# Loading the experts' first matrix in runs of 4 KB, with transposes of every second column

## The chip, the core and the metric

The kernel runs on one core of a Trainium2 chip. Its engines work side by side, each through its own queue in order: TensorE (PE; its weight loads are shown apart as PEld), VectorE (DVE), ScalarE (ACT), GpSimd (POOL) and SyncE (SP), which issues most DMAs. The metric is the device time of one execution in microseconds, as the median of several runs; less is better.

## The reference

The reference is one layer of a backbone over 1024 latent tokens of 1024 features, with 256 tokens of context. A first part mixes tokens (a gated recurrence and a spatial gating); it isn't touched. The second part is a mixture of experts, with 64 experts of which each token takes eight, and a shared expert that all tokens take:

```python
def swiglu(h, w_gu, w_down):
    gate, up = jnp.split(h @ w_gu, 2, axis=-1)
    return (jax.nn.silu(gate) * up) @ w_down

def expert_block(acc, blk):            # in moe_ffn, for each block of an expert's tokens
    tok, wts, e = blk
    out = swiglu(h_pad[tok], w_gu[e], w_down[e])
    return acc.at[tok].add(out * wts[:, None].astype(out.dtype)), None

return acc[:N] + swiglu(h, w_sh_gu, w_sh_down)
```

`w_gu[e]` is 1024 x 512 in f32 (gate and up side by side), `w_down[e]` 256 x 1024. All is float32.

## The kernel before

The token mixing fills roughly the first 920 us of the profile. Then come the units of the experts. The shared expert has eight units of 128 tokens; while they run, the routing is worked out: experts are ranked by how many tokens chose them, and each rank has a fixed number of rows, in tiles of at most 128, which gives 100 routed tiles, from 128 rows down to 16. Experts with many and with few rows alternate. Units with more than 128 rows have two tiles. The program is fixed; only the expert's number and the row indices are read at run time.

`step(n)` is a pipeline of three: the rows of unit n come in, unit n - 1 goes through the first matrix, unit n - 2 through the second.

*Weights.* `Weights.load` brings an expert in as six parts of 512 KB, four of `gu` (256 rows of 512 columns each) and two of `down`, into eight rotating buffers `er` of 128 partitions x 2 x 512. SyncE issues them, mostly in pairs, and waits for a buffer to be free; for the shared expert GpSimd issues them. `Weights.split` makes two tiles of each part, a rounded one `eh` (ScalarE, line 123) and the remainder `el` (VectorE, line 126), so that a product of f32 accuracy is three quick products: `eh` by the rounded rows, `el` by the rounded rows, `eh` by the rows' remainder (lines 1113 to 1115).

*Rows.* GpSimd gathers the rows of a tile by index from `h2x` in DRAM into `gx` (line 1092), 1088 values per row, the last 64 being the routing weights. VectorE takes the row's weight out of them (`wj`, line 1098), the first instruction that waits for the gather. `rows_in` transposes the 1024 features on TensorE, eight transposes of 128 columns each into `px` (line 1071), and splits the result into `x`, again with lines 123 and 126. In a transpose `gx` is the weight that is loaded and `ident` moves.

*Products.* `unit_up` accumulates over eight blocks k of 128 features. For a unit of up to 128 rows the weights' 512 columns move (lines 1113 to 1115); for a larger one the rows move (lines 1128 and 1129) and VectorE adds two halves of the result (`up`, line 1132). In the middle of it stands `mid`, which transposes the products of the unit before (`pt`, line 1147). `unit_down` multiplies with the second matrix (`pd`) and GpSimd adds the result to `acc` in DRAM with an indirect DMA (line 1166).

So on TensorE there follow one another: transposes of the next tile's rows, half of the products of the present unit, `pt` of the unit before, the other half, and `pd`. On VectorE `wj` of a coming tile stands ahead of parts of `el` and of the split `x`, so a gather that is late holds these up. On GpSimd adding and gathering DMAs alternate.

A contraction over 1024 features doesn't depend on which 128 of them stand in block k, as long as the rows of the weights and the columns that are transposed agree.

One other line reads with a step. Line 1373, in the routing, multiplies half-precision one-hot tiles that hold eight values side by side and takes one in eight, so that neighbouring columns lie 16 bytes apart:

```python
oa = ep.tile([P, NTT, 8], F16, name=f"oa{i}", tag="eh", bufs=12)
ob_ = ep.tile([P, P, 8], F16, name=f"ob{i}", tag="el", bufs=12)
TE.matmul(pix, ob_[:, :, k], oa[:, :, k], start=(i + k == 0), stop=(i == 7 and k == 7))
```

Of the kernel before, what the change touches and what calls it, by code (L numbers as in the profile page):

```python
# [18 lines left out]
DRAM = bass.MemoryType.DRAM  # L19
# [9 lines left out]
# experts, by descending count, with rows for more than 16 * j tokens  # L29
STEPS = (64, 64, 64, 63, 60, 53, 46, 39, 33, 28, 19, 15, 12, 10, 7, 7, 3, 3, 3, 2, 2, 1, 1, 1)  # L30
TSTEPS = STEPS[::8]  # and with more than j tiles of 128 rows
# [5 lines left out]
def layer(ctx: ExitStack, tc, x, c, cx, c_ctx, w_ada, b_ada, g_pre_mix, g_post_mix, g_pre_ffn, g_post_ffn, w_in,  # L37
# [14 lines left out]
    # tiles that pass from one phase to the other  # L52
# [43 lines left out]
    # vectors over features, one feature per partition  # L96
# [9 lines left out]
    def rsqrt(pool, ss, n, mul, nm):  # L106
        """1/sqrt(ss*mul + EPS) of a [128, n] tile: bit-level seed and three Newton steps."""
        v = pool.tile([P, n], F32, name=f"rv{nm}", tag="rv", bufs=3)
        i = pool.tile([P, n], I32, name=f"ri{nm}", tag="ri", bufs=3)
        y = pool.tile([P, n], F32, name=f"ry{nm}", tag="ry", bufs=4)  # L110
        t = pool.tile([P, n], F32, name=f"rt{nm}", tag="rt", bufs=3)
        V.tensor_scalar(v, ss, mul, EPS, op0=OP.mult, op1=OP.add)  # L112
        V.tensor_scalar(i, v.bitcast(I32), 1, None, op0=OP.arith_shift_right)  # L113
        V.tensor_scalar(y.bitcast(I32), i, -1.0, float(0x5F3759DF), op0=OP.mult, op1=OP.add)  # L114
        for _ in range(3):
            V.tensor_tensor(t, y, y, op=OP.mult)  # L116
            V.scalar_tensor_tensor(t, t, -0.5, v, op0=OP.mult, op1=OP.mult)  # L117
            V.scalar_tensor_tensor(y, t, 1.5, y, op0=OP.add, op1=OP.mult)  # L118
        return y
# [15 lines left out]
    # ================= phase 1 =================  # L135
# [85 lines left out]
    def ada_first(m, fill=iter(())):  # L221
        """Columns m * 512 and up of shift (m < 2) and scale (m >= 2), one feature per partition: the sum over each fourth of
        the rows goes to a group of columns of the tensor engine, where four run side by side."""
        ps = phg(f"pad_{m}")
        for k0 in (0, 4):
            was = [(t2 if m == 1 else pj)(f"wa{m}{k}") for k in range(k0, k0 + 4)]
            for g in range(4):
                last = SP.dma_start(was[g], w_ada[(k0 + g) * P:(k0 + g + 1) * P, m * 512:(m + 1) * 512])
            mm = None
            for g in (3, 0, 1, 2):  # L230
                with tc.issue_after(mm.ins) if mm else ExitStack():
                    i = TE.matmul(ps[32 * g:32 * g + 32], scl32[:, k0 + g], was[g], start=(k0 == 0), stop=(k0 == 4),
                                  tile_position=(0, 32 * g))
                mm = mm or i
            with tc.issue_after(i.ins):
                for _ in range(4):
                    next(fill, None)
        mrow = t2(f"mrow{m}")
        V.tensor_copy(mrow, ps)
        pada = ptr(f"pada{m}", (P, 4, 2))  # L240
        for j in range(4):
            TE.matmul(pada[:, j], mrow[:, j * P:(j + 1) * P], sel2, start=True, stop=True)
        n = m * 4
        for s in range(2):
            if m < 2:
                V.tensor_tensor(B1[:, n:n + 4, s], pada[:, :, s], vt[:, 24 + n:28 + n], op=OP.add)
            else:
                V.tensor_tensor(A1[:, n - 8:n - 4, s], pada[:, :, s], vt[:, 24 + n:28 + n], op=OP.add)
                V.tensor_tensor(A1[:, n - 8:n - 4, s], A1[:, n - 8:n - 4, s], vt[:, 8 + n:12 + n], op=OP.mult)
        return last.ins  # L250
# [6 lines left out]
    def wide(col, nm, al, kps=range(4)):  # L257
        """512 columns of w_in, split: [k] -> (h, l), each [128, 512]."""
# [50 lines left out]
    # in the order of need: half of the shifts and scales, of the modulated tokens and of the weights of the values, and the  # L309
    # products of these; the other halves  # L310
# [25 lines left out]
    def narrow(w, col, nm, nk=KB):  # L336
        """128 columns of w, split: h, l, each [128, nk, 128]."""
# [7 lines left out]
    def tokrows(w, si, i, nm):  # L345
        """[128 tokens, 512] of the modulated tokens times 512 columns of w_in."""
        ps = pmm(f"ps{nm}")
        for k in range(KB):
            tokpart(ps, w, si, i, k)
        return ps  # L350

    def featrows(hw, si, nm):
        """[128 features, tokens of a segment]."""
# [24 lines left out]
    # lower bounds: first entry of the softmax over two  # L378
# [32 lines left out]
    def sigmoids(h, r):  # L411
        """Forget gates to (sigmoid(z), sigmoid(-z)); query to silu."""
# [17 lines left out]
    def gates(hs, d, si, sp, sm, q):  # L430
        """Decayed keys and queries of 512 columns in one direction: one head's segment or two heads' context."""
# [16 lines left out]
        # chunk-level exponents within a block of 128: FQ, FK, L64, L32, Tot  # L448
# [31 lines left out]
        # keys decayed to the end of their chunk  # L480
# [31 lines left out]
    def to_block(g):  # L512
        """Keys decayed to the end of their block of 128, queries from its start, in place."""
# [14 lines left out]
    def scores(h, si, gf, gb):  # L528
        """A^T[s, t] of both directions for the four 128-blocks of a segment."""
# [40 lines left out]
    def hgrn(h, pr):  # L570
# [11 lines left out]
        # states before each block  # L582
# [146 lines left out]
    def gates_out(js):  # L729
        """Output gate of the recurrence (4 blocks) and gate of its branch (8 blocks), before their nonlinearities."""  # L730
# [115 lines left out]
    def choose(i, s_, r):  # L846
        """Chosen experts of a tile of tokens (mbf), how often each is chosen up to it (cum), and the weights."""
# [10 lines left out]
        # sum of the two largest of each group of eight  # L858
# [12 lines left out]
        # the four largest groups, then the eight largest experts, ties by index  # L871
# [10 lines left out]
        # weights of the chosen experts  # L882
# [8 lines left out]
    def out_x1(i, al):  # L891
        """The first sub-layer's residual of a tile of tokens."""
# [22 lines left out]
    def out_h2(i, x1, pool, sq):  # L915
        """The second sub-layer's input, in place."""
# [12 lines left out]
    def route_in(i, h2, wr, pr, tr, f, s_):  # L929
        """Scores of a tile of tokens."""  # L930
# [9 lines left out]
    def second():  # L940
        """All but the second half of the last tile; returns that."""
# [34 lines left out]
    # rows of each rank's slot, and its first row  # L976
# [28 lines left out]
    # ================= experts =================  # L1005
# [25 lines left out]
    class Weights:  # L1031
        """An expert's weights: gu [1024, 512] and down [256, 1024] in DRAM, in six parts, loaded and then split."""
# [5 lines left out]
        def load(self, n=6, q=SP):  # L1038
            for kp in range(self.nload, min(self.nload + n, 6)):
                raw = wp.tile([P, 2, 512], F32, name=f"er{self.nm}{kp}", tag="er", bufs=8)  # L1040
                if kp < 4:
                    last = q.dma_start(raw, self.gu(kp * 256, 256).rearrange("o (k p) f -> p (o k) f", p=P))
# [22 lines left out]
    def rows_in(gx, R, off, x2, nm):  # L1065
        """Rows of one tile, transposed and split, to columns off and up."""
        n = 4 if R > 64 else 8
        for k0 in range(0, KB, n):
            pt = epst(f"px{nm}{k0}")
            for k in range(n):  # L1070
                TE.transpose(pt[:, k * R:(k + 1) * R], gx[0:R, (k0 + k) * P:(k0 + k + 1) * P], ident[0:R, 0:R])  # L1071
# [5 lines left out]
    def unit_in(rows, slot, nm):  # L1077
        """Brings in the rows of a unit: (index column, number of rows) of its tiles; the second tile when told."""
# [27 lines left out]
    def unit_up(u, wg, nm, mid=None):  # L1106
        """silu(gate) * up of a unit's rows: by row for up to 128, else transposed."""
# [33 lines left out]
    def unit_act(u, a, nm):  # L1141
        """The products of a unit, transposed and split."""
# [28 lines left out]
    # units of rows, in order: the shared expert, which starts the sums, then the experts by descending count  # L1171
# [28 lines left out]
    def advance(s, n):  # L1200
        """The next n parts of an expert are split, and as many of the expert after it loaded."""
# [12 lines left out]
    def step(n):  # L1214
        """Rows of unit n come in, unit n - 1 goes up, unit n - 2 down."""
# [22 lines left out]
    # ================= routing, among the tiles of the shared expert =================  # L1238
# [50 lines left out]
    # positions within each expert, by token  # L1289
# [10 lines left out]
    # experts by descending count  # L1300
# [24 lines left out]
    # rows of each expert: its slot's tiles first, then blocks after all slots  # L1325
# [16 lines left out]
    # jump of the row number for positions past the slot  # L1342
# [20 lines left out]
    # tokens by row: products of one-hot rows and columns, eight of each token side by side  # L1363
# [17 lines left out]
    # expert and slot of each block past the slots  # L1381
# [25 lines left out]
    # the residual, for the end  # L1407
# [6 lines left out]
    # blocks past the slots, as many as the counts need  # L1414
# [14 lines left out]
    # ================= output =================  # L1429
# [39 lines left out]
```

## Time and profile before

| | |
|---|---|
| median of 3 runs | 2037.6 us |
| the three runs | 2026.79, 2037.6, 2038.34 us |
| span of the profiled execution | 2039.7 us |
| TensorE busy over the span | 1879.4 us (92%) |
| VectorE, ScalarE, GpSimd busy | 1303.0, 1081.4, 375.4 us |
| mean granted TensorE clock | 0.961 |
| moved by DMA | 412.95 MB, mean 202 GB/s |

The profiled execution is told by its span alone, from its first to its last instruction; it is one execution, and the times of the runs come from others. [...] A matmul that is shown as busy overlaps the next one, so that from its duration alone it isn't seen how quickly they follow each other.

### The profile page before, as it was taken

How to read it: one execution, taken by the hardware profiler on the slowest of the kernel's cores; microseconds unless marked ns; L12 is line 12 of the kernel's file. 1: busy time of each engine (PE TensorE's matmuls, PEld its weight loads, DVE VectorE, ACT ScalarE, POOL GpSimd, SP SyncE). 2: the span in 40 equal slices, each digit the busy share in tenths (PEclk: the TensorE clock that was granted, in tenths of full speed). 3: DMA queues.
4: the chain of work that ended last, by engine and by line, in shares of the span. 5: the costliest groups of instructions: out<-in, count | busy, mean ns of one | idle time of the engine just before them, and what ended most of it. 6: DMA issues, size and time to landing. Idle time of an engine off the chain costs nothing. (4 is left out here: it accounts for less than half of the span.)

```text
span 2039.7 us, 31209 instructions
## 1 busy us (share of the span) xinstructions
PE 1879.4 (92%) x10809; PEld 1493.2 (73%) x10810; DVE 1303.0 (64%) x2915; ACT 1081.4 (53%) x1823; POOL 375.4 (18%) x232
## 2 busy tenths in 40 slices
PE   6999999999999998998999999998999989999990
PEld 3787788878887776876677777776867777787770
DVE  5532867578535577778456776676756757576655
ACT  2437555364122225224447777676766767676652
POOL 0000000000000000000013344243433324432423
PEclk9999999999999998998899999999999989999995
DMA  9241212124016778444359999899989979899965
GB/s 325 84 124 42 63 63 74 58 68 128 19 31 205 227 247 260 154 151 158 128 179 295 315 302 299 238 316 282 295 256 276 320 236 318 285 286 297 322 187 185
DMA packets 224288, 412.95 MB, mean 202 GB/s; under 512 B 21624, under 2 KB 79544, under 8 KB 224128
## 3 DMA queue, kind: packets, MB, share of 16 engines
q1 hardware_dynamic: 199808, 336.70, 48.8%
q0 software_dynamic: 23488, 73.17, 14.7%
q8 instruction: 85, 1.39, 0.3%
q10 hardware_dynamic: 832, 1.08, 0.2%
q14 instruction: 75, 0.61, 0.1%
HBM read 351.18 MB, written 71.58 MB: 207 GB/s over the span
## 5 line engine op out<-in xcount | busy, mean ns | idle before, releaser
L126 DVE TENSOR_TENSOR el<-er,eh 128x1024 fp32r<-128x1024 f32 x384 | 458.0, 1219 | 52.1 <-ACT eh L123 47.2
L123 ACT CAST eh<-er 128x1024 fp32r<-128x1024 f32 x384 | 390.7, 1052 | 30.8 <-PE pg L1115 16.8
L1166 POOL DMA_INDIRECT acc<-y,idx x100 | 185.3, 1853 | 497.8 <-ACT y L1162 112.4
L1092 POOL DMA_INDIRECT gx<-h2x,idx x100 | 165.6, 1656 | 223.9 <-DVE idx L1380 102.0
L1162 ACT ACTIVATE y<-pd,wt 128x512 f32<-128x512 f32 (+7 forms) x200 | 136.9, 685 | 88.3 <-PE pd L133 46.2
L1113 PE MATMUL pg<-eh,x 128*128 128x512 f32 (+5 forms) x384 | 161.4, 420 | 0.0
L1114 PE MATMUL pg<-el,x 128*128 128x512 f32 (+5 forms) x384 | 153.5, 400 | 0.0
L1115 PE MATMUL pg<-eh,x 128*128 128x512 f32 (+5 forms) x384 | 153.5, 400 | 0.0
L1098 DVE SCALAR_TENSOR_TENSOR wj<-rank,gx 128x64 f32<-128x64 f32 (+7 forms) x100 | 21.7, 217 | 156.9 <-DMA gx<-h2x,idx 150.5
L1071 PEld LDWEIGHTS px<-ident,gx 128*128 128x128 f32 (+7 forms) x800 | 79.6, 140 | 22.4 <-issue 2.9
L1071 PE MATMUL px<-ident,gx 128*128 128x128 f32 (+7 forms) x800 | 90.0, 253 | 0.3
L555 POOL MEMSET dg<- 128x128 f32 x8 | 1.6, 205 | 461.4 <-PE pk L523 199.5
L1132 DVE TENSOR_TENSOR up<-pg,up 128x160 f32<-128x160 f32 (+5 forms) x104 | 34.8, 334 | 79.8 <-ACT up L1131 79.8
L1115 PEld LDWEIGHTS pg<-eh,x 128*128 128x128 f32 (+5 forms) x384 | 66.4, 173 | 24.5
L1113 PEld LDWEIGHTS pg<-eh,x 128*128 128x128 f32 (+5 forms) x384 | 67.1, 175 | 20.1
L1114 PEld LDWEIGHTS pg<-el,x 128*128 128x128 f32 (+5 forms) x384 | 67.0, 175 | 18.9
L131 PE MATMUL pd<-eh,swh 128*128 128x512 f32 (+5 forms) x192 | 76.0, 396 | 0.0
L133 PE MATMUL pd<-eh,swl 128*128 128x512 f32 (+5 forms) x192 | 75.7, 395 | 0.0
L132 PE MATMUL pd<-el,swh 128*128 128x512 f32 (+5 forms) x192 | 75.6, 394 | 0.0
L1186 POOL DMA_DIRECT2D sx<-h2x x1 | 0.8, 781 | 393.7 <-DVE rtz L117 393.7
L1131 ACT COPY up<-pg 128x160 f32<-128x160 f32 (+5 forms) x104 | 31.0, 298 | 56.4 <-PE pg L1129 55.6
L126 DVE TENSOR_TENSOR x<-px,x 128x512 fp32r<-128x512 f32 (+3 forms) x91 | 52.3, 613 | 10.2 <-ACT x L123 10.2
(1094 smaller groups left out, 5271.2 us busy)
## 6 DMA issues: line engine op xcount, KB each, us to landing
er<-in_w_expert_gu_dram SPq DMA_DIRECT2D x256, 512.0 KB
er<-in_w_expert_down_dram SPq DMA_DIRECT2D x128, 512.0 KB
wr_ad<-in_w_ada_dram SPq DMA_DIRECT2D x64, 256.0 KB
wa<-in_w_ada_dram SPq DMA_DIRECT2D x32, 256.0 KB
wrga<-in_w_in_dram SPq DMA_DIRECT2D x12, 512.0 KB
gsp<-go SPq DMA_DIRECT2D x24, 256.0 KB
wrc<-in_w_in_dram SPq DMA_DIRECT2D x8, 512.0 KB
wrf<-in_w_in_dram SPq DMA_DIRECT2D x8, 512.0 KB
```

Source lines behind the costliest of these rows:

```text
L123: A.copy(h, src)
L126: V.tensor_sub(l, src, h.bitcast(F32))
L131: TE.matmul(ps, ah, bh, start=(i == 0), stop=False)
L132: TE.matmul(ps, ah, bl, start=False, stop=False)
L133: TE.matmul(ps, al, bh, start=False, stop=(i == n - 1))
L1071: TE.transpose(pt[:, k * R:(k + 1) * R], gx[0:R, (k0 + k) * P:(k0 + k + 1) * P], ident[0:R, 0:R])
L1092: G.indirect_dma_start(out=gx[0:R], out_offset=None, in_=h2x, in_offset=bass.IndirectOffsetOnAxis(ap=ic[0:R], axis=0), bounds_check=T - 1, ...
L1113: TE.matmul(pg[0:C], ah, bh, start=(i == 0), stop=False)
L1114: TE.matmul(pg[0:C], ah, bl, start=False, stop=False)
L1115: TE.matmul(pg[0:C], al, bh, start=False, stop=(i == KB - 1))
L1162: A.activation(y[0:R, hf * 512:hf * 512 + 512], pd[0:R], AF.Copy, scale=1.0 if wt is None else wt[0:R])
L1166: G.indirect_dma_start(out=acc, out_offset=bass.IndirectOffsetOnAxis(ap=ic[0:R], axis=0), in_=y[0:R], in_offset=None, compute_op=OP.add, b ...
```

## The change

A part of `gu` is 256 rows of 2 KB that lie one behind the other in DRAM. Before, partition p takes rows p and 128 + p of the part, two runs of 2 KB. Now it takes rows 2p and 2p + 1, which are one run of 4 KB. The blocks k = 2 kp and 2 kp + 1 of the contraction thus hold the even and the odd features of 256 neighbouring ones, and the transposes take every second column to match. The same holds for the shared expert, whose weights and rows go through the same functions, and for the loop over blocks past the fixed tiles.

```diff
             for kp in range(self.nload, min(self.nload + n, 6)):
                 raw = wp.tile([P, 2, 512], F32, name=f"er{self.nm}{kp}", tag="er", bufs=8)
                 if kp < 4:
-                    last = q.dma_start(raw, self.gu(kp * 256, 256).rearrange("o (k p) f -> p (o k) f", p=P))
+                    last = q.dma_start(raw, self.gu(kp * 256, 256).rearrange("o (p k) f -> p (o k) f", p=P))
...
             for k in range(n):
-                TE.transpose(pt[:, k * R:(k + 1) * R], gx[0:R, (k0 + k) * P:(k0 + k + 1) * P], ident[0:R, 0:R])
+                c0 = (k0 + k) // 2 * 256 + k % 2
+                TE.transpose(pt[:, k * R:(k + 1) * R], gx[0:R, c0:c0 + 255:2], ident[0:R, 0:R])
```

Besides, comments are dropped, which moves line numbers by two behind this place. The instructions of each engine stand in the same order as before, one for one; what differs is the pattern that these loads and these transposes read.

## Rows read from the trace of the kernel before

**Rows 1.** Experts' stretch: PE, PEld, DVE, ACT, POOL busy; clock, DMA share, GB/s.

```profile
1030.00:1966.00 936.00, 883.25 (x4868) 705.35 (x4867) 634.76 (x1031) 646.80 (x1023) 340.75 (x193) 0.97 0.90 282
```

**Rows 2.** Waits of TensorE from 1050 us: total us, times, longest.

```profile
PE pt L1147 <- DVE x L126: 26.9, 12, 4.9
PE pg L1128 <- DVE up L1132: 20.5, 14, 2.8
PE pt L1147 <- DVE x__15325 L126: 4.9, 1, 4.9
```

**Rows 3.** Tile `er`: idle time of an engine before it, by what ended it.

```profile
  DMA er<-in_w_expert_down_dram: 0.3, 1
```

**Rows 4.** Waits of all engines: VectorE behind gathers; total us, times, longest.

```profile
DVE wj L1098 <- DMA gx<-h2x,idx: 150.5, 43, 8.2
```

**Rows 5.** Timeline around one late gather: start, us, instruction, idle before.

```profile
1383.69 2.08 POOL L1092 DMA_INDIRECT gx<-h2x,idx  x1 [0.30 <-PE pd L133]
...
1392.24 0.23 DVE L1098 SCALAR_TENSOR_TENSOR wj<-rank,gx 128x64 f32<-128x64 f32 x1 [7.40 <-DMA gx<-h2x,idx]
...
1394.27 0.58 PE L1147 MATMUL pt<-ident,sw 96*128 96x96 f32 x2 [4.55 <-DVE x L126]
```

**Rows 6.** TensorE in two short stretches: busy, granted clock, DMA share, GB/s.

```profile
974.20:977.00 2.80, 2.80 (x10) 0.50 0.93 285
1394.30:1397.00 2.70, 2.70 (x8) 0.50 0.97 272
```

**Rows 7.** DMA view, 960 to 962 us: packets; queue with packets, MB, share.

```profile
DMA packets 409, 0.77 MB, mean 386 GB/s; under 512 B 32, under 2 KB 32, under 8 KB 409
...
q1 hardware_dynamic: 409, 0.77, 99.9%
```

**Rows 8.** DMA view, 968 to 970 us.

```profile
DMA packets 222, 0.82 MB, mean 408 GB/s; under 512 B 23, under 2 KB 23, under 8 KB 222
...
q1 hardware_dynamic: 222, 0.82, 101.2%
```

**Rows 9.** Timeline of TensorE: groups of eight transposes with 96, 128, 16 rows.

```profile
1451.13 0.82 PE L1071 MATMUL px<-ident,gx 96*128 96x96 f32 x8
...
1463.83 1.03 PE L1071 MATMUL px<-ident,gx 128*128 128x128 f32 x8
...
1467.58 0.66 PE L1071 MATMUL px<-ident,gx 16*128 16x16 f32 x8
```

**Rows 10.** Matmuls by line and shape: busy us, mean ns, idle before.

```profile
L1071 PE MATMUL px<-ident,gx 128*128 128x128 f32 x376 | 48.7, 272 | 0.0
L1373 PE MATMUL small<-oa,ob 128*128 128x164 f16 x64 | 20.1, 477 | 0.0
L1071 PE MATMUL px<-ident,gx 96*128 96x96 f32 x80 | 9.1, 250 | 0.1
...
L1071 PE MATMUL px<-ident,gx 80*128 80x80 f32 x80 | 7.5, 234 | 0.1
L1071 PE MATMUL px<-ident,gx 112*128 112x112 f32 x56 | 6.5, 258 | 0.0
...
L1071 PE MATMUL px<-ident,gx 16*128 16x16 f32 x40 | 3.3, 211 | 0.0
```

**Rows 11.** Timeline of TensorE at three places: strided and dense products.

```profile
970.27 1.93 PE L1373 MATMUL small<-oa,ob 128*128 128x164 f16 x6
...
973.33 2.57 PE L1373 MATMUL small<-oa,ob 128*128 128x164 f16 x8
...
976.12 0.63 PE L1113 MATMUL pgs<-ehs,x2s 128*128 128x512 f32 x1
976.55 0.63 PE L1114 MATMUL pgs<-els,x2s 128*128 128x512 f32 x1
...
1504.17 0.39 PE L1113 MATMUL pg<-eh,x 128*128 128x512 f32 x1
1504.40 0.39 PE L1114 MATMUL pg<-el,x 128*128 128x512 f32 x1
```

## The prediction

> **What bounds the kernel now.** I began with the busy time of the experts' stretch, 1030 to 1966 us, because both edits act there. TensorE is busy for 883 of 936 us at a granted clock of 0.97 [rows 1]; the DMA engines are busy for 0.90 of it. Two resources near their limit, so the next views had to say which one the other waits for. Who waits for whom on TensorE: only two waits of weight, 26.9 us in 12 waits of `pt` behind VectorE's `x`, and 20.5 us in 14 waits of `pg` behind VectorE's `up` [rows 2]. No wait for a weight load is among them. The view of the tile `er`, into which the loads go, shows the other side: its first reader, ScalarE's cast, stood idle for the landing of such a load once, for 0.3 us [rows 3]. So the weight stream is early and TensorE sets the pace, interrupted when VectorE is late. Where VectorE is late it is often for a gather of rows: 150.5 us in 43 waits [rows 4]. One of them is followed through: at 1392.24 VectorE has waited 7.40 us for a gather, the split `x` of the previous rows stands behind it in VectorE's queue, and TensorE's `pt` starts after 4.55 us of idle time [rows 5], in a stretch whose granted clock from 1394.3 to 1397 is 0.50 [rows 6]. That chain is the only way I see by which a quicker weight stream can reach the end of the kernel.
>
> **The load.** 256 expert loads of 512 KB are changed (64 experts with four parts of `gu` each), and four of the shared expert's. Each goes from 256 runs of 2 KB to 128 runs of 4 KB. The price of both kinds of run can be read off two stretches in which SyncE's queue q1 has the engines to itself. From 960 to 962 us there are 409 packets, 32 of them under 512 B, so 377 runs in 0.77 MB, which is 2.04 KB each [rows 7]; 16 engines busy 99.9% of 2 us are 31.97 us, or 84.8 ns a run. From 968 to 970 us there are 222 less 23, so 199 runs in 0.82 MB, 4.1 KB each, in 32.4 us, or 163 ns a run [rows 8]. Two runs of 2 KB cost 170 ns and one of 4 KB 163: a saving of 7 ns, 4%. Over 256 loads it is 256 x 128 x 7 / 16 = 14 us of every DMA engine's time, in a stretch where the engines have about 94 us to spare already. Nobody waits for these landings, so by itself this is worth nothing on the path. SyncE issues the same number of DMAs in the same order. What it can do is let gathers land sooner. The gather followed above took 8.5 us from its issue at 1383.69 to its use; 4% of that is 0.35 us. TensorE waits behind VectorE's `x` 12 times, which makes 4 us. I take -4 us, with bounds of 0 (nothing lands sooner) and -30 (below, under the rivals).
>
> [...]
>
> **The transposes.** Each tile of rows is transposed by eight instructions in which 128 columns of `gx` are loaded as weights and the identity moves past them. The edit leaves their number and order; the 128 columns now lie 8 bytes apart, not 4. No operation of the trace reads so, thus bounds from the nearest rows. First what a transpose costs now, from groups of eight in a row on TensorE's timeline: with 128 rows eight last 1.03 us and the last one 0.272, so they follow each other at (1.03 - 0.272) / 7 = 0.108 us; with 96 rows at (0.82 - 0.25) / 7 = 0.081; with 16 rows at (0.66 - 0.211) / 7 = 0.064 [rows 9, 10]. With many rows the moving identity sets the pace; the floor of 0.064, which doesn't fall with the rows any more, I put down to the weight load.
>
> Then what a stride costs. One line has one: L1373 moves 164 half-precision columns that lie 16 bytes apart. Six take 1.93 us and one of them 0.477 (the mean of all), so they follow each other at 0.291 us; eight take 2.57 us from 973.33 on, so 0.299, and from 974.2 on the granted clock is 0.50 there [rows 6, 10, 11]. That is 1.8 ns a column. An ordinary product with 512 adjacent f32 columns follows the last one at 0.23 us (1504.17 to 1504.40), which is also 1.8 ns for 16 bytes, and at 0.43 us under the clock of 0.50 (976.12 to 976.55) [rows 6, 11]. So the strided read doesn't follow TensorE's clock and the dense one, away from the half clock, sits at the same 1.8 ns. Both fit an estimate: moving on by 16 bytes in a partition takes 1.8 ns, whatever part of them is used. For 128 f32 columns this is 32 steps and 0.058 us dense, just under the floor of 0.064, and 64 steps and 0.115 us at every second column; with the same 0.006 on top, 0.122 us a transpose.
>
> The sum by shape [rows 10]: with 128 rows 376, and 8 x 8 for the shared expert's tiles, are 440, at 0.122 - 0.108 = 0.014 us, 6.2 us; 56 with 112 rows at 0.027 (0.095 now, interpolated), 1.5; 80 with 96 rows at 0.041, 3.3; 80 with 80 rows at 0.052 (0.070 now, interpolated), 4.2; the shapes from 64 rows down to 16, which are what is left of the 100 routed tiles with 8 each, 800 - 376 - 56 - 80 - 80 = 208, at 0.058, 12.1. That is 27 us on TensorE's own queue. The lower bound is 0, since the load may go on at its present pace; a gain I exclude, as no read gets shorter. The upper bound is the strided row itself, 1.8 ns for every column: 0.236 us a transpose, and 126 us in all. I take the 27, as the two rates that I divide by agree and one of them is a f32 read.
>
> Not all of it lengthens the kernel. A tile's transposes stand ahead of its `pt`, and in 26 of the 100 routed tiles TensorE waits behind VectorE anyway [rows 2], at 27 / 108 = 0.25 us a tile: 6.5 us vanish in these waits, and I allow 10, as a later TensorE also finds VectorE further on in the tile after. The rest has no cover. What is late next is nothing new: ScalarE and VectorE, with 647 and 635 us busy of 936 [rows 1], have room.
>
> **Sum.** 27 - 10 - 4 = +13 us on the profiled span of 2039.7 us, so 2053. The three timed runs lie at 2026.8 to 2038.3 with the median at 2037.6, 2 us under the span, which makes the forecast **2051 us**. Its own range comes from 20 to 33 us of added reads, 5 to 15 under waits, and 0 to 8 of earlier gathers: 2035 to 2064.
>
> **Rivals.**
> First: two columns out of 16 bytes come as fast as four, and the transposes cost nothing. [...] Against it: the match of the 1.8 ns. Then only the -4 us are left, 2034 us (2026 to 2040). [...]
>
> Second: the DMA engines bound the stretch after all, through the latency of gathers and of the adding writes. For it: a DMA share of 0.90 over the whole stretch [rows 1] and the 150.5 us of VectorE waiting [rows 4]. Against it: no reader of the weights waits for them [rows 3], and the saving is 4%. It pays the 14 us of engine time and half of the 32 us that TensorE waits behind `x` (26.9 in `pt` and 4.9 in one more [rows 2]): -30 us, and with some cost of the transposes left 2012 us (2005 to 2022).
>
> Third, and slower: a run of 4 KB holds a DMA engine for 163 ns and not 85, and a gathered row that shares the engine has to let one or two of them by. A tile of 128 rows is 8 rows an engine: 8 x 78 ns = 0.6 us a gather with one run between two rows, 1.25 us with two. It decides if a queue of weight loads is full whenever a gather runs, so that the number of runs let by stays and not the bytes. 43 waits times 0.6 to 1.25 are 27 to 54 us more on VectorE, of which TensorE sees about a fifth today (32 of 150.5), 6 to 11 us. In place of the -4 it makes +23 to +28, and with stretches at half clock behind the longer waits 2066 us (2058 to 2085). Against it: SyncE issues loads in pairs, and a gather mostly waits until what is queued has gone.
>
> **Chances.** The forecast 0.46; first rival 0.23; second 0.17; third 0.14, with the dear end of the stride (126 us) in it at 0.03. The likeliest case gives the time. The range of 2014 to 2070 leaves out half of the second rival and over half of the third, 0.16 together. A measurement of this kernel tells about 1% (20 us) from no change. Faster by more: 0.14, nearly all the second rival. Slower by more: 0.25, the upper quarter of the forecast and most of the third. Within 1%: 0.61.
>
> **What the profile after would show.** Weight loads of `px` at about 0.20 us where they are 0.140 now, and eight transposes of a tile with 16 rows over about 1.07 us, not 0.66: that decides between the forecast and the first rival (which leaves both). Runs of the weight queue: 128 per load instead of 256, DMA share down by one or two hundredths. VectorE's waits for gathers near 150 us: under 110 would speak for the second rival, above 180 for the third. What would make me wrong is a stride that costs per column, or half-clock stretches that move with small shifts of the waits, each of which is worth some us.

## The result, and the profile after

The changed kernel takes 2063.5 us (median of 4 runs, 2063.1 to 2068.3); the kernel before, on the same chip, 2038.0. The ratio is 1.0135, with a 95% interval of 1.0099 to 1.0171: slower by 1.4%, 26 us. The forecast was 2051 us, and the range of 2014 to 2070 holds the result. It will turn out that this was luck: the term that was to cost did not, and the term that was to save cost 28 us.

Did the transposes get dearer? The page's group of weight loads (busy us, mean ns, idle before), before and after, then TensorE's timeline after (start, us, instruction) and the matmuls by shape:

```profile
L1071 PEld LDWEIGHTS px<-ident,gx 128*128 128x128 f32 (+7 forms) x800 | 79.6, 140 | 22.4 <-issue 2.9
```

```profile
L1073 PEld LDWEIGHTS px<-ident,gx 128*128 128x128 f32 (+7 forms) x800 | 109.1, 209 | 17.6 <-issue 2.9
```

```profile
1476.57 1.11 PE L1073 MATMUL px<-ident,gx 128*128 128x128 f32 x8
1480.41 1.12 PE L1073 MATMUL px<-ident,gx 16*128 16x16 f32 x8
```

```profile
L1073 PE MATMUL px<-ident,gx 128*128 128x128 f32 x376 | 52.3, 282 | 0.0
...
L1073 PE MATMUL px<-ident,gx 16*128 16x16 f32 x40 | 5.6, 269 | 0.0
```

With 16 rows they follow each other at (1.12 - 0.269) / 7 = 0.122 us where it was 0.064 [rows 9, 10], with 128 rows at (1.11 - 0.282) / 7 = 0.118 where it was 0.108. The forecast was 0.122 for both, so it is met almost to the nanosecond: the number of rows hardly matters any more, and I put the pace down to the weight load, whose mean went from 140 to 209 ns.

And the load? Two microseconds in which the weight queue has the engines to itself, in the view of DMA queues after:

```profile
DMA packets 212, 0.77 MB, mean 387 GB/s; under 512 B 23, under 2 KB 23, under 8 KB 212
...
q1 hardware_dynamic: 212, 0.77, 100.1%
```

189 runs of 4 KB where there were 377 of 2 KB [rows 7], for the same 0.77 MB: 32.0 us / 189 = 169 ns a run, which is what two runs of 2 KB cost. The small packets in these views are charged to the runs, so a difference of 7 ns can't be resolved here. Over the whole program the pages tell it better (queue: packets, MB, share of 16 engines), before and after:

```profile
q1 hardware_dynamic: 199808, 336.70, 48.8%
```

```profile
q1 hardware_dynamic: 167040, 336.70, 47.5%
```

48.8% of 2039.7 us are 995 us of every engine, 47.5% of 2066.5 are 982: 14 us less, as the prediction had it, for 32768 runs fewer. So the long runs do save engine time, and still the kernel is slower. No reader of `er` waited for a load. Yet TensorE's waits behind `x` have grown (total us, times, longest), and VectorE's for gathers are about as they were [rows 2, 4]:

```profile
PE pt L1149 <- DVE x L126: 38.3, 12, 5.6
PE pg L1130 <- DVE up L1134: 13.7, 10, 1.7
PE pd L131 <- ACT y L1164: 4.9, 2, 3.9
```

```profile
DVE wj L1100 <- DMA gx<-h2x,idx: 147.6, 40, 8.6
```

The late gather that the prediction followed [rows 5] has its twin here, and this time the timeline is read with one more row, ScalarE's:

```profile
1392.83 2.07 POOL L1094 DMA_INDIRECT gx<-h2x,idx  x1 [0.30 <-PE pd L133]
1399.01 0.68 ACT L1164 ACTIVATE y<-pd,wt 32x512 f32<-32x512 f32 x1 [5.72 <-DMA acc<-y,idx]
1399.65 1.59 POOL L1168 DMA_INDIRECT acc<-y,idx  x1 [4.75 <-DMA acc<-y,idx]
...
1401.61 0.23 DVE L1100 SCALAR_TENSOR_TENSOR wj<-rank,gx 128x64 f32<-128x64 f32 x1 [7.64 <-DMA gx<-h2x,idx]
...
1403.63 0.58 PE L1149 MATMUL pt<-ident,sw 96*128 96x96 f32 x2 [4.61 <-DVE x L126]
```

VectorE waits for the gather at `wj`. But ScalarE too stands idle, for 5.72 us, until an earlier adding write (`acc<-y`) has read the buffer `y`; behind it in ScalarE's queue is the cast of `x`, which VectorE's split needs. Two transfers hold up TensorE here, and the prediction had looked at one: the cast ran from 1401.11 to 1402.14 and VectorE's split from 1402.89 on, so the gather was the later of the two by under a microsecond. This one place is hardly later than before: the gather takes 8.78 us to its use where it took 8.55, and TensorE waits 4.61 us where it waited 4.55 [rows 5]. In the kernel before the same row of ScalarE is there, unread:

```profile
1389.35 0.68 ACT L1162 ACTIVATE y<-pd,wt 32x512 f32<-32x512 f32 x1 [5.27 <-DMA acc<-y,idx]
```

To compare equal work I take the stretch from the first transpose of gathered rows to the last product of the down step: some 4970 matmuls in each kernel. The view by windows (length, then busy PE, PEld, DVE, ACT, POOL, clock, DMA share, GB/s), before and after:

```profile
1032.70:1989.00 956.30, 900.66 (x4970) 718.43 (x4969) 637.50 (x1038) 653.96 (x1037) 344.88 (x195) 0.97 0.90 281
```

```profile
1028.00:2017.40 989.40, 928.17 (x4969) 749.76 (x4968) 639.02 (x1038) 657.90 (x1037) 335.44 (x196) 0.96 0.86 271
```

TensorE: 27.5 us more busy, and 61.2 us idle where it was 55.6. Up to here my theory was the prediction's: the strided reads cost this. It took one run of each half to overturn it.

### The profile page after: what moved, and what is told of

It is laid out like the page before. It is cut to its first block, busy times and chain, and to the rows that moved or that the text cites. A ratio compares the mean times of both kernels' runs of the same rounds, so it can differ in the third digit from the quotient of the medians.

```text
span 2066.5 us, 31209 instructions
## 1 busy us (share of the span) xinstructions
PE 1901.6 (92%) x10809; PEld 1520.5 (74%) x10810; DVE 1304.3 (63%) x2915; ACT 1085.4 (53%) x1823; POOL 363.7 (18%) x232
## 3 DMA queue, kind: packets, MB, share of 16 engines
q1 hardware_dynamic: 167040, 336.70, 47.5%
## 5 line engine op out<-in xcount | busy, mean ns | idle before, releaser
L123 ACT CAST eh<-er 128x1024 fp32r<-128x1024 f32 x384 | 391.8, 1051 | 38.7 <-PE pg L1117 25.5
L1094 POOL DMA_INDIRECT gx<-h2x,idx x100 | 156.2, 1562 | 235.1 <-PE px L1073 107.6
L1073 PEld LDWEIGHTS px<-ident,gx 128*128 128x128 f32 (+7 forms) x800 | 109.1, 209 | 17.6 <-issue 2.9
L1073 PE MATMUL px<-ident,gx 128*128 128x128 f32 (+7 forms) x800 | 112.2, 282 | 0.2 <-DVE x__15325 L126 0.2
```

The source lines that it names most:

```text
L123: A.copy(h, src)
L1073: TE.transpose(pt[:, k * R:(k + 1) * R], gx[0:R, c0:c0 + 255:2], ident[0:R, 0:R])
L1094: G.indirect_dma_start(out=gx[0:R], out_offset=None, in_=h2x, in_offset=bass.IndirectOffsetOnAxis(ap=ic[0:R], axis=0), bounds_check=T - 1, ...
```

## Experiments: which half of the change costs

The two halves apart: `e1` loads runs of 4 KB and transposes as before; `e2` transposes with a stride and loads as before.

```
e1:  last = q.dma_start(raw, self.gu(...).rearrange("o (p k) f -> p (o k) f", p=P))
     TE.transpose(..., gx[0:R, (k0 + k) * P:(k0 + k + 1) * P], ident[0:R, 0:R])
e2:  last = q.dma_start(raw, self.gu(...).rearrange("o (k p) f -> p (o k) f", p=P))
     c0 = (k0 + k) // 2 * 256 + k % 2
     TE.transpose(..., gx[0:R, c0:c0 + 255:2], ident[0:R, 0:R])
```

> The loads in runs of 4 KB, the transposes of neighbouring columns as before; the features then stand against the wrong rows of the weights, so only its time is read. My theory, that the strided weight loads of the transposes cost the 25 us and the load moves nothing on the path: 2032 to 2041 us, transposes 0.109 us apart with 128 rows and 0.062 with 16. Rival, that the 4 KB runs hold back gathers: 2055 to 2066 us, VectorE's waits for gathers above 180 us. Rival, that the runs save time which the transposes hide: 2010 to 2025 us.

> The transposes of every second column, the loads in two runs of 2 KB as before; features and weight rows don't agree, so only its time is read. My theory: the whole loss, 2060 to 2070 us, transposes 0.120 us apart at every number of rows. If the 4 KB runs cost: 2038 to 2048 us. If they save 10 us or more: 2073 us or above.

Measured: `e1` 2064.8 us, ratio 1.0141 (1.0102 to 1.0181); `e2` 2037.9 us, ratio 0.9985 (0.9957 to 1.0013). The whole loss is the load's; the stride costs nothing that can be measured. TensorE's waits behind `x` in `e1`, and in `e2`:

```profile
PE pt L1148 <- DVE x L126: 39.3, 12, 5.6
```

```profile
PE pt L1149 <- DVE x L126: 25.6, 9, 5.8
```

They are the wait that goes with the load: 38.3 and 39.3 us with runs of 4 KB (the changed kernel and `e1`), 26.9 and 25.6 with 2 KB (the kernel before and `e2`). The stretch of equal work in `e1`, and in `e2`:

```profile
1027.50:2009.00 981.50, 910.07 (x4970) 725.78 (x4969) 637.46 (x1038) 654.38 (x1037) 337.27 (x196) 0.96 0.87 273
```

```profile
1030.90:1995.10 964.20, 922.78 (x4970) 744.74 (x4969) 639.21 (x1038) 658.61 (x1037) 347.93 (x196) 0.97 0.89 278
```

`e2` has the 22.1 us of dearer transposes (922.78 - 900.66) and 14.2 us less idle time (41.4 for 55.6): it fits that TensorE works while it would have waited. The other 8 us are less than the 10 us by which single executions differ either way. `e1` has 15.8 us more idle time and 9.4 us more busy time for the same matmuls, at a granted clock of 0.96, not 0.97.

Two more forms of these edits. `e3` reads every fourth column, 16 bytes apart. `e4` loads 4 KB and stores the rows of `h2x` with even features first, so that the transposes read adjacent columns.

```
e3:  c0 = (k0 + k) // 4 * 512 + k % 4
     TE.transpose(..., gx[0:R, c0:c0 + 509:4], ident[0:R, 0:R])
e4:  eo = lambda a: a.rearrange("p (q i j) -> p q j i", q=2, j=2)
     V.tensor_tensor(x1[hf].rearrange("p (q j i) -> p q j i", q=2, j=2), eo(sq), eo(B2[hf]), op=OP.add)
```

> Loads as before, transposes of every fourth column, 16 bytes apart; only its time is read, as the features don't agree with the weights. By 1.8 ns for each 16 bytes that a weight load passes, a transpose takes 128 x 1.8 + 6 = 236 ns; summed over the shapes 126 us more than before, of which none was absorbed in the changed kernel: 2150 to 2170 us. If the strided load costs a fixed amount whatever the step: 2060 to 2070 us. If twice the step costs twice the addition: about 2090 us.

> Loads in runs of 4 KB; the rows of the second part are written to memory with the even features of each 256 ahead of the odd ones, so that the transposes read neighbouring columns; the router's matrix is loaded to match. Complete. My theory: like the loads alone, 2030 to 2045 us, with up to 5 us more for 16 VectorE additions that read with a step ahead of the experts. If 4 KB runs save time: 2010 to 2025 us, which beats both kernels. If they hold back gathers: 2055 us or above.

Measured: `e3` 2042.7 us, ratio 1.0012 (0.9986 to 1.0039); `e4` 2063.4 us, ratio 1.0115 (1.0081 to 1.0149). `e4`, a complete kernel without strided transposes, says again that the load costs it all; TensorE's wait behind `x` is 38.5 us there and 26.3 in `e3`. `e3` contradicts the rate by which I had sized the stride, as its timeline shows:

```profile
1466.77 1.13 PE L1073 MATMUL px<-ident,gx 16*128 16x16 f32 x8
```

(1.13 - 0.268) / 7 = 0.123 us with one column in 16 bytes, as with two; by 1.8 ns for every 16 bytes it would be 0.236.

## Experiments: is it the length of the run?

The new theory is the third rival's, with the adding writes beside the gathers: their rows share the 16 DMA engines with the weight queue, and each row lets a weight run by. How long such a transfer takes is in the view of DMA issues (line, count, median us from issue to landing; 1030 to 1990 us). With 2 KB (`e2`) and with 4 KB (`e1`):

```profile
gx<-h2x,idx POOLq DMA_INDIRECT x97, 8.6
acc<-y,idx POOLq DMA_INDIRECT x97, 7.6
```

```profile
gx<-h2x,idx POOLq DMA_INDIRECT x96, 9.5
acc<-y,idx POOLq DMA_INDIRECT x96, 8.6
```

0.9 us more a gather and 1.0 us more an adding write. But these are medians of one execution each, and this pair lies among the farthest apart. In the changed kernel itself, with 4 KB, the same rows are nearer to those with 2 KB:

```profile
gx<-h2x,idx POOLq DMA_INDIRECT x97, 8.8
acc<-y,idx POOLq DMA_INDIRECT x95, 8.4
```

If the length of the run is the cause, shorter runs must give time back, and the second matrix (128 of the 384 loads, in 4 KB all along) must count as the first does.

```
f1:  first matrix, four runs of 1 KB: src = self.gu(...).rearrange("o r (h f) -> o (r h) f", h=2)
f2:  second matrix, two runs of 2 KB (the indices of its blocks are swapped to match):
     self.down(0, 256)[:, :, (kp - 4) * 512:(kp - 3) * 512].rearrange("o (j p) f -> p (o j) f", p=P)
f3:  both    f4:  the load of e1, and the second matrix as in f2
```

> The kernel before with contiguous transposes; each part of the experts' first matrix is loaded in four runs of 1 KB per partition where there were two of 2 KB. The quarter rows fall on other partitions, so the features don't match and this is for its time alone. Theory (the rows of gathers and of adding writes wait on their DMA engine until the weight run ahead has gone, so their delay grows with the length of that run): 2 KB to 4 KB cost 26 us for these loads and lengthened a run by 78 ns; 2 KB to 1 KB shortens it by about 40 ns, so about 13 us are given back, 2024 us, ratio 0.993; VectorE's waits for gathers fall below 147 us. Rival, engine time counts (twice the runs, each with a fixed part): DMA share rises from 0.90, gathers come later, ratio 1.005 to 1.02. Rival, the length of a run is not what matters, but that neighbouring rows go to one partition, or that small shifts move the stretches at half clock: ratio within 0.997 to 1.003.

> The kernel before, with the second matrix loaded by halves of its columns, 256 rows by 512 columns a part, in 256 runs of 2 KB; before it was 128 whole rows a part, in 128 runs of 4 KB. Complete. Theory (delay by the length of the run): these are 128 of the 384 expert loads, half of those that cost 26 us when they went from 2 to 4 KB, so 13 us come back: 2024 us, ratio 0.993 to 0.994; the gather's waits on VectorE fall from 150 us, TensorE's waits behind x too. Rival, engine time counts: 128 x 128 x 7 ns / 16 = 7 us more of every DMA engine, ratio 1.000 to 1.005. Rival, the pairing of neighbouring rows or chance: no such pairing is touched, ratio within 0.997 to 1.003.

> Both edits together: first matrix in runs of 1 KB, second in runs of 2 KB, contiguous transposes. The features don't match, for its time alone. Theory: the two gains add, about 2011 us, ratio 0.987. Rival, engine time counts: 1.01 to 1.03. Rival, pairing or chance: within 0.997 to 1.003.

> First matrix in runs of 4 KB as in the kernel after, with contiguous transposes, and the second in runs of 2 KB. The features don't match, for its time alone. Theory: 26 us lost by the one, 13 come back by the other, so half of the loss of the load alone: 2051 us, ratio 1.006 to 1.007. Rival, the pairing of neighbouring rows is what costs: the full loss stays, 2064 us, ratio 1.014. Rival, engine time counts: fewer runs for the one, more for the other, ratio under 1.000 if this were all.

| run | first / second matrix | gather, add: median us to landing | rows of an add: mean us from first to last | ratio (95%) |
|---|---|---|---|---|
| e1 | 4 KB / 4 KB | 9.5, 8.6 | 3.88 | 1.0141 (1.0102 to 1.0181) |
| after | 4 KB / 4 KB | 8.8, 8.4 | 3.82 | 1.0135 (1.0099 to 1.0171) |
| e4 | 4 KB / 4 KB | 9.3, 8.4 | 3.80 | 1.0115 (1.0081 to 1.0149) |
| f4 | 4 KB / 2 KB | 9.2, 8.1 | 3.68 | 1.0077 (1.0052 to 1.0102) |
| e3 | 2 KB / 4 KB | 8.5, 7.9 | 3.56 | 1.0012 (0.9986 to 1.0039) |
| e2 | 2 KB / 4 KB | 8.6, 7.6 | 3.57 | 0.9985 (0.9957 to 1.0013) |
| before | 2 KB / 4 KB | not in its view | 3.50 | 1 |
| f2 | 2 KB / 2 KB | 8.6, 7.8 | 3.54 | 0.9999 (0.9974 to 1.0024) |
| f1 | 1 KB / 4 KB | 8.5, 8.0 | 3.53 | 0.9968 (0.9946 to 0.9991) |
| f3 | 1 KB / 2 KB | 8.3, 8.1 | 3.51 | 0.9970 (0.9952 to 0.9988) |

(`after`, `e2` and `e3` have strided transposes besides.) `f4` came out as the theory says: half of the loss goes when only the other matrix gets shorter runs, though no pair of rows of the first is parted. So the pairing of rows is not what costs, or not all of it. `f1` has the sign, at half the size, and its interval holds the rival's 0.997 but not the theory's 0.993. `f2` and `f3` miss: beside runs of 2 KB or 1 KB, the second matrix' runs cost nothing. So three of the four results lie nearer to the rival than to the theory, and the price doesn't follow the bytes in long runs in proportion. Why not stays open.

The landing times part the runs that lose time (gathers at 8.8 us and more) from the others (8.6 and less), but don't order them: the changed kernel has 8.8 and loses more than `f4` with 9.2, and the adds of `f1` and `f3`, at 8.0 and 8.1, are as late as those of `f4`. A closer sign is in the traces' records of single DMA packets, which the views above only sum up. An adding write moves one packet of 4096 bytes a row on queue q0. The fourth column has the mean time from the start of its first row to the end of its last, over the 94 writes that move any rows, 8192 rows in each run. With 2 KB it is 3.5 to 3.6 us, with 4 KB 3.8 to 3.9, with `f4` between them, and below 2 KB it gains nothing, where the times gain 0.3% at most. An estimate by the third rival, one run of 78 ns more between two rows on an engine, is 8192 / 94 / 16 x 78 ns = 0.4 us; it measured 0.3. The time from issue to the end of the last row grows by less, from 7.2 to 7.4 us, and it is 7.4 in `f1` and `f3` too; so how 0.3 us a transfer become 26 us of the kernel isn't shown by it.

Engine time did fall with longer runs, to a DMA share of 0.87 in `e1` from 0.92 in `f1`, whose stretch of equal work is

```profile
1030.80:1987.10 956.30, 905.48 (x4969) 721.47 (x4968) 637.44 (x1038) 655.03 (x1037) 343.29 (x196) 0.97 0.92 281
```

But hardly a reader waits for these loads (0.3 us in the kernel before [rows 3]), and here each step to shorter runs was faster or made no difference.

## Experiments: through what does it reach TensorE?

If late gathers and adds carry the price, it must go when nobody waits for them any more. First the gathers: a fourth buffer `gx`, for which the high halves of the weights give up one of twelve. With 2 KB (`g1`), and with 4 KB (`g2`).

```
-    NG = 3
+    NG = 4
-                h = ep.tile([P, 2, 512], F32R, name=..., tag="eh", bufs=12)
+                h = ep.tile([P, 2, 512], F32R, name=..., tag="eh", bufs=11)
```

> The kernel before with four buffers for gathered rows where there were three (and, to make room, 11 of 12 buffers for the high halves of the weights), so that a gather goes out about one tile sooner. Complete. Theory (gathers that land late hold up VectorE, and TensorE behind it): VectorE's waits for gathers fall from 150 us to under 90, TensorE's waits behind x from 32 us to under 20, 2020 to 2033 us, ratio 0.991 to 0.998. Rival, the adding writes and the waits of one for the other carry the cost: the gathers' waits fall and the time stays, ratio 0.998 to 1.003. Rival, one weight buffer less is what counts: slower, ratio over 1.003.

> Four buffers for gathered rows as in the run before it, with the first matrix loaded in runs of 4 KB and contiguous transposes; the features don't match, for its time alone. It is read against the same kernel with runs of 2 KB. Theory (late gathers carry the price of the long runs): with the gathers out a tile sooner most of the 1.4% is gone, this one within 0.5% of the one with 2 KB. Rival, the adding writes carry it (each waits for the one before, and gathers stand behind them): the difference stays at 1.2 to 1.5%. Rival, the price is not in the latency of either: the same, 1.2 to 1.5%, with the gathers' waits on VectorE short in both.

Measured: `g1` 2010.2 us, ratio 0.986 (0.982 to 0.990), a complete kernel that beats both and lies below its theory's 2020 to 2033 us; `g2` 2031.4 us, 0.9977 (0.9951 to 1.0004). Between them 1.1%, nearer to the rivals' 1.2 to 1.5% than to the theory's 0.5%: the price is not mainly in VectorE's waits for gathers. Those are nearly gone in `g1`, and the others are not (waits, 1030 to 1990 us):

```profile
DVE wj L1098 <- DMA gx<-h2x,idx: 14.2, 8, 5.5
```

```profile
PE pt L1147 <- DVE x L126: 22.5, 8, 4.5
```

```profile
ACT y L1162 <- DMA acc<-y,idx: 60.9, 15, 7.9
```

```profile
POOL acc L1166 <- DMA acc<-y,idx: 145.0, 27, 8.6
```

150.5 us of waiting for gathers [rows 4] became 14.2, and TensorE still waits 22.5 us behind `x`. ScalarE now waits longer for `y`, 60.9 us (38.7 in the kernel before), and GpSimd's adding writes 145.0 us (105.1) for the one before. The rows of an add are spread over 3.61 us in `g1` and 3.99 in `g2`. So the adding writes were next: each waits for the one before it, as all go to one array. In `h1` (2 KB) and `h2` (4 KB) they go in turn to two.

```
+    acc2 = dr.tile([T, D], F32, name="acc2")
...
-                G.indirect_dma_start(out=acc, ...
+                acount[0] += 1
+                G.indirect_dma_start(out=(acc, acc2)[acount[0] % 2], ...
```

> Four buffers for gathered rows as in g1, runs of 2 KB, and the adding writes go in turn to two arrays of sums, so that none waits for the one just before it; the second array is left out of the output, so this is for its time alone. Theory (what is left of the price of long runs passes through the adding writes: each waits for the one before, ScalarE waits for the buffer y, and the casts of weights stand behind it): GpSimd's waits of an add for an add fall from 145 us to under 60, ScalarE's wait for y from 61 us to under 40, and the time to 1990 to 2008 us, ratio 0.976 to 0.985. Rival, the adding writes are hidden: 2010 us, ratio 0.986 as g1.

> As h1, with the first matrix in runs of 4 KB (the features don't match, and the second array of sums is left out; for its time alone). It is read against h1. Theory (gathers and adding writes together carry the price of the long runs): with both out of the way the 4 KB cost under 0.4%. Rival, something else than the latency of these two (TensorE's half clock, VectorE's or ScalarE's own work, the landing of the weights): the 1.1% that was left between g2 and g1 stays, 0.9 to 1.3%.

Measured: `h1` 1958.9 us, ratio 0.9593 (0.9560 to 0.9626); `h2` 1955.2 us, ratio 0.9584 (0.9553 to 0.9616). The price of the 4 KB is gone: the difference is 0.1%, in favour of the long runs, inside both intervals. And `h1` gained far more than expected. First the two waits that it was to shorten (145.0 and 60.9 us in `g1`), both far below what was expected, then TensorE's waits, all that are over 0.1 us, and the stretch of equal work:

```profile
POOL acc L1171 <- DMA acc<-y,idx: 7.1, 4, 3.0
```

```profile
ACT y L1165 <- DMA acc<-y,idx: 18.9, 12, 3.3
```

```profile
PE pd L131 <- ACT y L1165: 2.0, 2, 1.5
PE pos L1398 <- DVE scr L1396: 1.3, 1, 1.3
PE pg L1129 <- DVE up L1133: 0.2, 1, 0.2
```

```profile
1030.40:1910.70 880.30, 876.35 (x4970) 700.99 (x4968) 641.37 (x1039) 655.87 (x1038) 366.29 (x195) 1.00 0.97 308
```

4 us idle of 880, and a granted clock of 1.00. `h2`:

```profile
1028.30:1905.20 876.90, 874.19 (x4970) 699.92 (x4969) 641.09 (x1039) 655.96 (x1038) 367.17 (x195) 1.00 0.95 309
```

The transfers themselves are no quicker: gathers land after 8.6 us (`h1`) and 8.9 (`h2`), adds after 8.8 and 9.1. They still land later beside long runs, as far as one execution of each tells, and TensorE no longer waits for it. Not tried: two arrays with three gather buffers; adding the second array into the output, which costs something at the end; the strided reads where TensorE has no idle time left to take them in.

## Why the prediction was right in its range and wrong in its sum

- **The range held by luck.** The sum has +17 us for transposes that cost nothing in the end and -4 for a load that costs 28; 13 us in all against 26 measured. 2063.5 us is just inside the forecast's own 2035 to 2064 (whose terms, 33 - 5 us, would reach 2066).
- **What bounds the kernel: half right.** TensorE sets the pace and no reader of weights waits. That a late gather is the only way from the weight stream to the end was wrong: with the gathers' waits nearly gone, a price of 1.1% is left (`g2` to `g1`). The adding writes, which only the second rival names, are another way, with a row of waiting of their own that I did not read.
- **The load, -4 us: the step that failed.** The saving in engine time was right, 14 us. The step from there was wrong: that a lower price per byte lets the gather land sooner by as much. Alone the load costs 28 us (`e1`); gathers land at 8.8 to 9.5 us with 4 KB and 8.5 or 8.6 with 2 KB, adds at 8.4 to 8.6 and 7.6 to 7.9, and TensorE's waits behind `x` grew from 26.9 to 38.3 us.
- **The transposes on TensorE's queue, +27 us: right in size, wrong in reason.** 0.122 us each came out, and 22 us in sum (`e2`). But 1.8 ns for every 16 bytes is no law of this read, since `e3`, at 0.123 us, pays no more for twice the step. The first rival, that two columns of 16 bytes come as fast as four, failed for the pace of the transposes; that they cost no time was right, for another reason.
- **What of them lies under waits, 10 us: failed.** The time of `e2` shows none of the 27. TensorE's idle time shrank by 14 in the profile. I counted cover only in the tiles where TensorE waits today; the fall in idle time is larger than the 6.5 us that gave.
- **The third rival had the sign and, for a part, the size.** 0.6 to 1.25 us a gather was forecast; by medians of single executions it was 0.2 to 0.3 us in the changed kernel and 0.9 to 1.0 in `e1`. It counted no adds, and passed a fifth of the waits on to TensorE, 6 to 11 us. Its 2066 us came close because 17 us of transposes that cost nothing made up for a load that costs 28. What I held against it, that a gather mostly waits until the queue has gone, doesn't fit transfers that land later beside longer runs.
- **Its sign in the profile was badly chosen.** VectorE's waits for gathers were to pass 180 us; they are 147.6, and in kernels with 2 KB they vary from 126.0 (`e2`) to 150.5. Such a wait also depends on how early VectorE comes. TensorE's waits behind `x`, 38.3 us for 26.9, were the better sign.

**Shown:** the loss is the load's (`e1`, `e2`, `e4`); beside a first matrix in 4 KB it halves with shorter runs of the second (`f4`); with four gather buffers a difference of 1.1% is left, and with two arrays for the adding writes on top it is gone (`g1` to `g2`, `h1` to `h2`). So it passes through waits that these two changes remove together; two arrays with three gather buffers were not run. **Argued only:** that a row waits for a whole weight run at its engine. The spread of an add's rows fits it, `f1` to `f3` limit it. Nor is the way from the adds to TensorE seen in the waits from 1030 to 1990 us: with 4 KB (`after`, `e1`, `e4`) ScalarE waits 25.7 to 32.9 us for `y`, less than the 36.2 to 41.3 with 2 KB (`before`, `e2`, `e3`), and GpSimd's waits of an add for an add, 98.5 to 130.4 us, overlap the 100.1 to 115.3 with 2 KB.

## What to carry to other kernels

Before lengthening the runs of a stream that nobody waits for, look at the short, row-wise transfers that share its DMA engines: take their landing time, from more than one execution, and find who waits for it on every engine, including whoever waits for a source buffer to come free. A chain of adding writes into one array is such a waiter; two arrays were worth more here (`h1` against `g1`, 2.6%, without the last addition) than any size of run. Cost added to an engine that waits some thirty times in a stretch, as TensorE here, can be paid out of its waits, so size it against all of its idle time before adding it to the span.

## What the runs showed of the hardware

- Transposes of 16 rows, which I put down to the load of 128 f32 columns, follow each other at 0.064 us when the columns are adjacent, at 0.122 when they lie 8 bytes apart (`after`) and at 0.123 at 16 bytes (`e3`). So two columns in 16 bytes and one cost the same here, nearly twice the adjacent read.
- Row-wise transfers on one queue were slower here beside longer runs on another: with a second matrix in 4 KB, gathers land after a median of 8.5 us beside first-matrix runs of 1 KB (`f1`), 8.5 and 8.6 beside 2 KB (`e3`, `e2`), 8.8, 9.3 and 9.5 beside 4 KB (`after`, `e4`, `e1`). The rows of an adding write are spread over 3.5 us, 3.5 to 3.6 and 3.8 to 3.9.
- TensorE's granted clock over the experts' stretch was 0.97 with 55.6 us of idle time in pieces (before), and 1.00 with 4.0 us (`h1`). The same 4970 matmuls took 900.7 and 876.4 us. After the 4.55 us of idle time in [rows 5] the granted clock was 0.50 [rows 6], where it had been 1.00 from 1380 to 1389.6 us. So gaps were paid a second time here: 52 us of idle time went, and 24 us of busy time went with them.
